# Gated three-branch decoder layer on one core: cross attention's scale moved to ScalarE, another PSUM bank for the index keys, split halves at the start, new product order, shifted tables

## The chip, the cores and the metric

The kernel runs on one core of a Trainium2 chip. TensorE multiplies (PE in the profile; PEld is its weight load), VectorE (DVE), ScalarE (ACT) and GpSimd (POOL) do elementwise work, and SyncE (SP) issues most transfers. The metric is the device time of one execution in microseconds, lower is better.

## What is computed

One decoder layer on 256 tokens of width 1024: h = rmsnorm(x), z = h @ w_in, and z is cut into the inputs of three mixers and their gates.

```
A: ya = moba_attention(rope(mq), rope(mk), mv)        8 heads of 64, causal
B: yb = dsa_attention(rope(dq), rope(dk), dv, index)  8 heads of 64; the index scores pick 64 keys per token
     score = sum over 8 index heads of relu(iq . ik / 8) * iw, causal; top 64
C: yc = cross_attention(xq, xk, xv)                   4 heads of 128 over 256 memory tokens
     xk, xv from rmsnorm(mem) @ w_mem_kv;  p = softmax(q . k / sqrt(128))
u   = sum over A, B, C of sigmoid(gate logits + b) * (w_up @ (y * silu(g)))
out = rmsnorm(x + u @ w_out)
```

With 256 tokens mixer A's past blocks are empty, so A is plain causal attention.

## The kernel before, in words

**Products.** Each fp32 operand is kept as a high part (a cast to fp32r) and a low part (the rest), and a product is three matmuls: high by high and the two mixed ones (`product`, L252 to L256). The work is a list of some 100 steps. A step is 512 KB of weights, computed in two halves, `mm(w, 0)` and `mm(w, 1)`, with side work allowed in the middle (the main loop, L988 to L1001). A step of `gemm` (blocks mv, i0, i1, dv, xv: 5 blocks of 4 steps) has the activations as PE's stationary operand, the weights as the moving one and two accumulators, one for each 128 tokens; a half step is 6 matmuls, three into the one accumulator, then three into the other. The other blocks (`gemm_k`, `gemm_t`, `gemm_kv`, `gemm_u`) hold the weights stationary. The program opens with steps 0 to 7, in which mv (even) and mq (odd) take turns.

**Weights.** For step s the SP queue loads `w{s}r` six steps ahead (four buffers; w3r goes on ACT's queue). `split_weights` (L240) makes the two parts three steps ahead: `w{s}h` is a cast on ACT (L248), `w{s}l` a subtraction on DVE (L249); five buffers of each. Steps 0 and 1 (`HALVED = 2`) are split in halves of 128x512, all others in one 128x1024 piece.

**Side work.** Attention, rotations, evacuations and normalisations stand at places in the list, as a step number with or without .5: `IDX` (index transpositions, index heads, top-k rounds), `TURNS` (load of a swapped copy and rotation of queries and keys), `M_PAIRS`, `D_PAIRS`, `X_HEADS` (heads of A, B, C), `GATES`, `MEM` (loads of the memory tokens), `LOAD_ROWS` (the token rows, for the norm), `ORDER` (the order of the weight blocks). The order of PE's and POOL's instructions is that of the program text. On ACT, DVE and SP a scheduler sets it from dependencies and places, so moving a place moves other instructions too.

**The parts touched.**

- `idx_transpose(t)` (L444), at steps 27.5 and 28.5. PE transposes the index queries in two groups of four (`iqt`, L454), ACT copies each to `iqT` (L455); then PE transposes the keys (`ikt`, L458) and DVE copies them to `ikT` (L459). All three PSUM tiles have the tag `sc`, which has two banks that are also used by attention scores (`msc`, `dsc`, `xsc`) and index heads (`lg`).
- `tp` is one bank, for the transpositions of probabilities: `mtp`, `dtp` (L626), `xpt` (L681).
- `self_values` (L641, `mya`): PE multiplies values by the transposed probabilities; their high part `mph` comes from ACT (L627), the low part `mpl` from DVE (L628). `self_scale` (L617) scales the probabilities `mpr` on POOL before they are transposed.
- `cross_scores` (L649): score, row maximum on DVE (L658, L659), two exponentials on ACT with row sums (L663). `cross_scale` (L669): reciprocal of the sums on DVE (L671), then a multiplication of each 128x256 half of `xpr` by it on POOL (L673). `cross_transpose` (L675): PE transposes to `xpt`. Four heads, so eight multiplications.

Of the kernel before, what the change touches and what calls it, by code (L numbers as in the profile page):

```python
# [9 lines left out]
F32R = mybir.dt.float32r  # L10
AF = mybir.ActivationFunctionType
# [3 lines left out]
P = 128  # L15
S = 256
# [46 lines left out]
HALVED = 2  # L63
ORDER = (
# [4 lines left out]
)  # L69
LOAD_ROWS = 1  # L70
X_STATS = 6

IDX = (27.5, 30, 35)

TURNS = (('mq', 8.5, 15.5), ('mk', 13.5, 20.5), ('dq', 28, 33), ('dk', 33, 36))

M_PAIRS = ((23, 25.5), (24, 27.5), (26.5, 29.5), (29.5, 31.5))
D_PAIRS = ((43.5, 47.5), (46.5, 49.5), (51.5, 53.5), (54.5, 55.5))
X_HEADS = (41.5, 44.5, 49, 50.5)
GATES = 59.5  # L80

MEM = (1.5, 6, 11, 15, 21.5)


def block_places(blocks, nk):
# [8 lines left out]
class Steps:  # L94
# [11 lines left out]
    def at(self, step, fn, *args):  # L106
        self.side[step].append((fn, args))
# [3 lines left out]
def hybrid_layer_kernel(  # L111
# [14 lines left out]
    nc = tc.nc  # L126
# [5 lines left out]
    psum = ctx.enter_context(tc.tile_pool(name="psum", bufs=1, space=bass.MemoryType.PSUM))  # L132
# [6 lines left out]
    def k4(nm, dt=F32):  # L139
        return keep.tile([P, 4, S], dt, name=nm, tag="t4", bufs=6)  # L140
# [99 lines left out]
    def split_weights(s):  # L240
        raw = loaded.pop(s)
        shape = list(raw.shape)
        hi = ws.tile(shape, F32R, name=f"w{s}h", tag="whi")
        lo = ws.tile(shape, F32R, name=f"w{s}l", tag="wlo")
        part = 1 if s < HALVED else shape[1]
        for j in range(0, shape[1], part):
            ks = slice(j, j + part)
            last_hi[0] = nc.scalar.copy(hi[:, ks, :], raw[:, ks, :]).ins  # L248
            nc.vector.tensor_sub(lo[:, ks, :], raw[:, ks, :], hi[:, ks, :].bitcast(F32))  # L249
        halves[s] = (hi, lo)  # L250

    def product(ps, a, b, first, last):  # L252
        (ah, al), (bh, bl) = a, b
        nc.tensor.matmul(ps, ah, bh, start=first, stop=False)
        nc.tensor.matmul(ps, ah, bl, start=False, stop=False)
        nc.tensor.matmul(ps, al, bh, start=False, stop=last)  # L256

    accs = {}
# [5 lines left out]
    def acc_tiles(nm):  # L264
        accs[nm] = [acc_bank(f"{nm}_{t}") for t in range(2)]

    def gemm(nm, act, src, place, nk=NK):

        off, n = place
        plan.first[nm] = len(plan.steps)  # L270
        for k0 in range(0, nk, 2):

            def mm(w, half, k0=k0):
                if k0 + half == 0:
                    acc_tiles(nm)
                a = act()
                for kk in (half,):
                    k = k0 + kk
                    for t in range(2):
                        tok = slice(t * P, (t + 1) * P)  # L280
                        product(
                            accs[nm][t][:, :n], (a[0](k, tok), a[1](k, tok)),
                            (w[0][:, kk, :], w[1][:, kk, :]), k == 0, k == nk - 1,
                        )

            plan.add((src, off, nk, n, k0, 2), mm)
        plan.end[nm] = len(plan.steps)
# [156 lines left out]
    def idx_transpose(t):  # L444
        if t == 0:
            idx["q"] = [k4(f"iqT{j}", F32R) for j in range(2)]
            idx["k"] = keep.tile([P, 2, S], F32R, name="ikT", tag="ikT")
            for nm in ("sel", "acc", "wk"):
                idx[nm] = keep.tile([P, 3 * P], F32, name=nm, tag=nm)
        tok = slice(t * P, (t + 1) * P)  # L450
        for j in range(2):
            tp = psum.tile([P, 4, P], F32R, name=f"iqt{t}{j}", tag="sc", bufs=2)
            for g in range(4):
                nc.tensor.transpose(tp[:, g, :], idx["qs", t][:, 4 * j + g, :], ident_r)  # L454
            nc.scalar.copy(idx["q"][j][:, :, tok], tp)  # L455
        tp = psum.tile([P, 2, S], F32R, name=f"ikt{t}", tag="sc", bufs=2)
        for j in range(2):
            nc.tensor.transpose(tp[:, j, 0:P], idx["ks", t][:, j, :], ident_r)  # L458
        nc.vector.tensor_copy(idx["k"][:, :, tok], tp[:, :, 0:P])  # L459
# [209 lines left out]
    def cross_scale(hd):  # L669
        pr, st = prs["x", hd]  # L670
        nc.vector.reciprocal(st[:, 4:6], st[:, 2:4])  # L671
        for t in range(2):
            nc.gpsimd.tensor_scalar_mul(pr[:, t, :], pr[:, t, :], st[:, 4 + t : 5 + t])  # L673

    def cross_transpose(hd):  # L675
        pr, _ = prs["x", hd]
# [178 lines left out]
    for t in range(2):  # L855
        at(IDX[0] + t, idx_transpose, t)
    for g in range(NH):
        at(IDX[1] + g / 2, idx_head, g)
    for r in range(TOPK // 8):
        at(IDX[2] + r, idx_round, r)  # L860
    at(IDX[2] + TOPK // 8, idx_select)
    for nm, swap, turn in TURNS:
        for hf in range(2):
# [7 lines left out]
    def attend(nm, starts, bias):  # L871
        for b, (s0, s1) in enumerate(starts):
            at(s0, self_scores, nm, b, bias)
            for e in range(2):
                at(s0 + 0.5 + 0.5 * e, self_scale, nm, 2 * b + e)
                at(s1 + e, self_transpose, nm, 2 * b + e)
                at(s1 + 1 + e, self_values, nm, 2 * b + e)

    attend("m", M_PAIRS, lambda: bias_c)
    attend("d", D_PAIRS, lambda: idx["sel"])  # L880

# [32 lines left out]

    at(LOAD_ROWS, load_rows)
    at(X_STATS, start_stats)
# [10 lines left out]

    for pair, s0 in enumerate(MEM[0:4]):
        at(s0, mem_load, pair)
# [4 lines left out]

    at(MEM[4], mem_stats)
    at(MEM[4] + 2, rstd_rows, m_rstd, mB, "mB")
    for hf in range(2):
# [3 lines left out]
    for hd, h0 in enumerate(X_HEADS):  # L941
        at(h0, cross_scores, hd)
        at(h0 + 0.5, cross_scale, hd)
        at(h0 + 2, cross_transpose, hd)
        at(h0 + 3.5, cross_values, hd)
# [16 lines left out]
    n = len(plan.steps)  # L962
# [18 lines left out]
    for s in range(-SPLIT_AHEAD, n):  # L981
        p, rest = divmod(s + SPLIT_AHEAD, 2)
        if p < 4 and not rest:
            first[p]()
        if s == 4:
            nc.sync.dma_start(cst, consts[:, 0:512])
            nc.sync.dma_start(tabT.rearrange("p t c -> p (t c)"), consts[:, 512:1024])
        for fn, args in plan.side.pop(s, []):  # L988
            fn(*args)
        if LOAD_AHEAD <= s + LOAD_AHEAD < n:  # L990
            load_weights(s + LOAD_AHEAD)
        if s + SPLIT_AHEAD < n:
            split_weights(s + SPLIT_AHEAD)
            if s + SPLIT_AHEAD == 0:
                load_late()
        if s >= 0:
            w = halves.pop(s)
            plan.steps[s][1](w, 0)
            for fn, args in plan.side.pop(s + 0.5, []):
                fn(*args)  # L1000
            plan.steps[s][1](w, 1)  # L1001
# [64 lines left out]
```

## Time and profile before

| | |
|---|---|
| runs, median (lowest to highest) | 330.37 us (329.61 to 330.69) |
| the profiled execution | 328.81 us, of which 327.0 us is the span of instructions |
| PE busy | 314.1 us, 96% of the span |
| DVE, ACT, POOL busy | 253.2 (77%), 199.3 (61%), 67.8 us (21%) |
| granted TensorE clock, mean | 0.994 |
| DMA | 59.45 MB, mean 182 GB/s |

The span is the time from the first to the last instruction in the trace; the 1.81 us between it and the execution's own time lie outside. A timeline row has start, duration, engine, line, operation, output and inputs, and in brackets the engine's idle time before it and what ended it. Matmuls overlap: the distance between two starts tells more than the duration.

### The profile page before, as it was taken

To read this page: it belongs to the slowest core of one execution; us is meant where nothing else is said; L and a number is where in the kernel's file an instruction comes from. 1 tells how busy PE (TensorE), PEld (TensorE's weight loads), DVE (VectorE), ACT (ScalarE), POOL (GpSimd) and SP (SyncE) were. 2 spreads that over 40 slices of the span, in tenths; PEclk is the share of its full clock that TensorE was granted. 3 is DMA by queue.
4 is the path that set the end of the run, shared out by engine and by line. 5 is a ranking of instruction groups with operands and counts; after the bars stand their busy time and mean duration, and the time that the engine had idled before them with its cause. 6 is when DMAs were issued, how large, how long until landed. Compare 5 with 4: busy or idle time off the path is not lost. (4 is left out here: it accounts for less than half of the span.)

```text
span 327.0 us, 6396 instructions
## 1 busy us (share of the span) xinstructions
PE 314.1 (96%) x2442; PEld 298.8 (91%) x2442; DVE 253.2 (77%) x456; ACT 199.3 (61%) x347; POOL 67.8 (21%) x66
## 2 busy tenths in 40 slices
PE   8899999999899999979999999999999999999992
PEld 7799999999799989869999998999999999999882
DVE  3579999998789999978766659999577677467523
ACT  5699565697777645275656586756444556644433
POOL 0001000039413000064423464231001011015011
PEclk9999999999999999999999999999999999999997
DMA  7998795846737266664434433468656666646003
GB/s 210 377 346 297 230 292 182 284 141 221 195 102 193 71 180 201 188 199 130 133 124 126 134 123 86 147 238 312 202 186 192 192 175 178 204 159 191 2 0 128
DMA packets 18368, 59.45 MB, mean 182 GB/s; under 512 B 2209, under 2 KB 2465, under 8 KB 18337
## 3 DMA queue, kind: packets, MB, share of 16 engines
q1 hardware_dynamic: 17760, 57.73, 56.1%
q10 hardware_dynamic: 576, 1.31, 1.1%
q8 instruction: 19, 0.31, 0.4%
q14 instruction: 13, 0.10, 0.1%
HBM read 55.89 MB, written 1.05 MB: 174 GB/s over the span
## 5 line engine op out<-in xcount | busy, mean ns | idle before, releaser
L617 POOL TENSOR_SCALAR mpr<-mpr,mst 128x128 f32<-128x128 f32 (+1 forms) x16 | 17.9, 1134 | 52.5 <-DVE mst L615 52.5
L744 POOL TENSOR_TENSOR u<-u,gt 128x512 f32<-128x512 f32 x7 | 10.7, 1529 | 76.0 <-DVE gt L741 76.0
L673 POOL TENSOR_SCALAR xpr<-xpr,xst 128x256 f32<-128x256 f32 x8 | 9.2, 1164 | 53.2 <-DVE xst L671 53.2
L617 POOL TENSOR_SCALAR dpr<-dpr,dst 128x128 f32<-128x128 f32 (+1 forms) x16 | 15.0, 956 | 16.2 <-DVE dst L615 16.2
L731 ACT ACTIVATE gt<-gt,x_first 128x256 f32<-128x256 f32 x24 | 10.9, 501 | 3.9 <-DVE gt L728 3.9
L607 ACT ACTIVATE dpr<-dms,dst 128x128 f32<-128x128 f32 (+1 forms) x16 | 7.1, 448 | 6.2 <-DVE dst L603 6.2
L663 ACT ACTIVATE xpr<-xsc,xst,xs_rstd 128x256 f32<-128x256 f32 x8 | 4.4, 561 | 6.9 <-DVE xst L659 6.9
L607 ACT ACTIVATE mpr<-mms,mst 128x128 f32<-128x128 f32 (+1 forms) x16 | 7.1, 445 | 1.8 <-DVE mst L603 1.8
L785 ACT ACTIVATE junk<-xn 128x512 f32<-128x512 f32 (+1 forms) x5 | 2.7, 543 | 8.6 <-DVE xn L783 8.6
L904 POOL COPY bias_c<-cst 128x128 f32<-128x128 f32 x1 | 1.0, 1037 | 25.5 <-DMA cst<-consts 25.5
L789 POOL TENSOR_TENSOR xn<-xn,gf 128x512 f32<-128x512 f32 x2 | 2.6, 1288 | 16.3 <-ACT junk L785 16.3
L749 ACT CAST us<-u 128x512 fp32r<-128x512 f32 x4 | 2.5, 622 | 5.1 <-POOL u L744 3.4
L485 ACT ACTIVATE rl<-lg 128x384 f32<-128x384 f32 x8 | 3.9, 484 | 2.7 <-issue 2.1
L647 DVE TENSOR_TENSOR dyT<-dyT,dya 64x256 f32<-64x256 f32 x8 | 3.3, 417 | 2.6 <-ACT dyT L646 2.5
L965 PE MATMUL warm<-ones 128*128 128x128 f32 x18 | 4.2, 430 | 1.0 <-DVE eps_t L960 1.0
L488 DVE SCALAR_TENSOR_TENSOR acc<-rl,iw,acc 128x128 f32<-128x128 f32 (+1 forms) x14 | 5.2, 414 | 0.0
L646 ACT COPY dyT<-dya 64x256 f32<-64x256 f32 x8 | 2.9, 366 | 3.6 <-PE dya L641 3.4
L603 DVE CUSTOM_DVE_ANT_0 mms<-msc,bias_c 128x128 f32<-128x128 f32 (+1 forms) x16 | 5.0, 348 | 0.0
L481 PE MATMUL lg<-ikT,iqT 128*128 128x128 f32 (+1 forms) x32 | 5.0, 278 | 0.0
L603 DVE CUSTOM_DVE_ANT_0 dms<-dsc,sel 128x128 f32<-128x128 f32 (+1 forms) x16 | 4.8, 354 | 0.2
L185 ACT ACTIVATE ehi<-eT,x_first 128x256 fp32r<-128x256 f32 x8 | 3.6, 505 | 2.1 <-DMA eT<-memT 2.1
L965 PEld LDWEIGHTS warm<-ones 128*128 128x128 f32 x18 | 3.9, 331 | 1.0 <-DVE eps_t L960 1.0
(1296 smaller groups left out, 1547.7 us busy)
## 6 DMA issues: line engine op xcount, KB each, us to landing
x_rows<-x SPq DMA_DIRECT2D x2, 512.0 KB, 6.9
eT<-memT SPq DMA_DIRECT2D x4, 256.0 KB, 4.6
xn<-x SPq DMA_DIRECT2D x2, 512.0 KB, 4.8
w0r<-w_in SPq DMA_DIRECT2D x2, 256.0 KB, 3.6
w1r<-w_in SPq DMA_DIRECT2D x2, 256.0 KB, 5.0
xT<-xT SPq DMA_DIRECT2D x2, 256.0 KB, 6.5
w2r<-w_in SPq DMA_DIRECT2D x1, 512.0 KB, 7.0
w3r<-w_in ACTq DMA_DIRECT2D x1, 512.0 KB, 7.0
```

The lines of the kernel that those rows point to most:

```text
L185: nc.scalar.activation(hi[:, k, :], src, AF.Copy, scale=g)
L481: nc.tensor.matmul(lg[:, c : c + n], q[:, q0:q1], idx["k"][:, j, 0:n], start=j == 0, stop=j == 1)
L485: nc.scalar.activation(rl, lg[:, : 3 * P], AF.Relu, scale=HD**-0.5)
L488: nc.vector.scalar_tensor_tensor(acc[:, c], rl[:, c], iw[:, t, g : g + 1], (bias_c if g == 0 else acc)[:, c], op0=OP.mult, op1=OP.add,)
L603: nc.vector.tensor_tensor_reduce(out=ms[:, c], in0=sc[:, c], in1=bias()[:, c], op0=OP.add, op1=OP.min, scale=-(HD**-0.5), scalar=3e38, acc ...
L607: big["last_exp"] = nc.scalar.activation(pr[:, c], ms[:, c], AF.Exp, bias=st[:, t : t + 1], scale=-1.0, accum_out=st[:, 2 + t : 3 + t],)
L617: nc.gpsimd.tensor_scalar_mul(pr[:, c], pr[:, c], st[:, 4 + t : 5 + t])
L663: big["last_exp"] = nc.scalar.activation(pr3[:, t, :], sc[:, t, :], AF.Exp, bias=st[:, t : t + 1], scale=xs_rstd[:, t : t + 1], accum_out= ...
L673: nc.gpsimd.tensor_scalar_mul(pr[:, t, :], pr[:, t, :], st[:, 4 + t : 5 + t])
L731: nc.scalar.activation(gt[:, f, :], gt[:, f, :], AF.Sigmoid, bias=x_first[:, j : j + 1])
L744: adder.tensor_tensor(u, u, gt, op=OP.add)
L965: nc.tensor.matmul(warm[:, 0:P], ones, ones, start=True, stop=True)
```

## The change

1. Cross attention's probabilities are scaled by ACT instead of POOL.
2. The PSUM tile `ikt` of the index keys takes the tag `tp` instead of `sc`.
3. The weights of steps 2 and 3 are split in halves, as those of 0 and 1 are.
4. In `gemm` a half step computes high by high for both accumulators, then high by low weights for both, then low by high weights for both.
5. Tables: the index work starts half a step (transpositions), one step (heads) and one and a half steps (rounds) earlier; rotations of dq come 3 steps earlier, of dk 1.5 later; the second and third pair of mixer B's heads start later by 1 and 0.5 and are transposed earlier by 0.5 and 0; the token rows are loaded 3 steps earlier, the memory's first two pairs later by 0.5 and 1; u20 comes after u03 and l22 before l23.

```diff
-LOAD_ROWS = 1
+LOAD_ROWS = -2
-IDX = (27.5, 30, 35)
+IDX = (27, 29, 33.5)
-D_PAIRS = ((43.5, 47.5), (46.5, 49.5), (51.5, 53.5), (54.5, 55.5))
+D_PAIRS = ((43.5, 47.5), (47.5, 49), (52, 53.5), (54.5, 55.5))
...
@@ split_weights
-        part = 1 if s < HALVED else shape[1]
+        part = 1 if s < HALVED + 2 else shape[1]
@@ gemm
-                for kk in (half,):
-                    k = k0 + kk
+                k = k0 + half
+                for i, (p, q) in enumerate(((0, 0), (0, 1), (1, 0))):
                     for t in range(2):
-                        tok = slice(t * P, (t + 1) * P)
-                        product(
-                            accs[nm][t][:, :n], (a[0](k, tok), a[1](k, tok)),
-                            (w[0][:, kk, :], w[1][:, kk, :]), k == 0, k == nk - 1,
+                        nc.tensor.matmul(
+                            accs[nm][t][:, :n], a[p](k, slice(t * P, (t + 1) * P)),
+                            w[q][:, half, :], start=k + i == 0, stop=k + i == nk + 1,
                         )
@@ idx_transpose
-        tp = psum.tile([P, 2, S], F32R, name=f"ikt{t}", tag="sc", bufs=2)
+        tp = psum.tile([P, 2, S], F32R, name=f"ikt{t}", tag="tp", bufs=1)
@@ cross_scale
-            nc.gpsimd.tensor_scalar_mul(pr[:, t, :], pr[:, t, :], st[:, 4 + t : 5 + t])
+            nc.scalar.activation(
+                pr[:, t, :], pr[:, t, :], AF.Copy, scale=st[:, 4 + t : 5 + t]
+            )
```

What the tables move is seen in the order of the instructions, at three places.

PE, first index transposition (`iqt`, `ikt`), before: it stands behind the first half of step 27 of block dk0.

```order
L254 MATMUL dk0ps<-xhi,w27h 128x256
L255 MATMUL dk0ps<-xlo,w27h 128x256
L256 MATMUL dk0ps<-xhi,w27l 128x256
L454 MATMUL iqt_1167<-ident_r,iqs_931 128x128 x4
L454 MATMUL iqt_1173<-ident_r,iqs_931 128x128 x4
L458 MATMUL ikt_1179<-ident_r,iks_932 128x128 x2
L641 MATMUL mya_1085<-mph_1092,mv 128x256
L641 MATMUL mya_1085<-mpl_1093,mv 128x256
L641 MATMUL mya_1085<-mph_1092,mv 128x128
L641 MATMUL mya_1085<-mpl_1093,mv 128x128
L626 MATMUL mtp_1191<-cst,mpr_977 128x128 x3
L254 MATMUL dk0ps<-xhi,w27h 128x256
```

Now it stands ahead of step 27:

```order
L254 MATMUL dk0ps<-xhi,w26h 128x256
L255 MATMUL dk0ps<-xlo,w26h 128x256
L256 MATMUL dk0ps<-xhi,w26l 128x256
L453 MATMUL iqt_1150<-ident_r,iqs_935 128x128 x4
L453 MATMUL iqt_1156<-ident_r,iqs_935 128x128 x4
L457 MATMUL ikt_1162<-ident_r,iks_936 128x128 x2
L254 MATMUL dk0ps<-xhi,w27h 128x256
L255 MATMUL dk0ps<-xlo,w27h 128x256
L256 MATMUL dk0ps<-xhi,w27l 128x256
```

The transposition of the index moved by one half step, away from the product `mya` and the transposition `mtp` of mixer A, which it used to precede directly.

DVE, around the first low part `mpl` of mixer A's probabilities, which PE's `mya` reads (`w..l` are low parts of weights, `mst` row sums), before:

```order
L249 TENSOR_TENSOR w27l<-w27r,w27h 128x1024
L615 RECIPROCAL mst_976<-mst_976 128x2
L249 TENSOR_TENSOR w28l<-w28r,w28h 128x1024
L615 RECIPROCAL mst_983<-mst_983 128x2
L628 TENSOR_TENSOR mpl_1045<-mtp_1046,mph_1044 128x384
L249 TENSOR_TENSOR w29l<-w29r,w29h 128x1024
L249 TENSOR_TENSOR w30l<-w30r,w30h 128x1024
L647 TENSOR_TENSOR myT<-myT,mya_1085 64x256
L628 TENSOR_TENSOR mpl_1093<-mtp_1094,mph_1092 128x384
```

and now:

```order
L249 TENSOR_TENSOR w28l<-w28r,w28h 128x1024
L614 RECIPROCAL mst_980<-mst_980 128x2
L614 RECIPROCAL mst_987<-mst_987 128x2
L249 TENSOR_TENSOR w29l<-w29r,w29h 128x1024
L627 TENSOR_TENSOR mpl_1049<-mtp_1050,mph_1048 128x384
L249 TENSOR_TENSOR w30l<-w30r,w30h 128x1024
L646 TENSOR_TENSOR myT<-myT,mya_1089 64x256
L627 TENSOR_TENSOR mpl_1097<-mtp_1098,mph_1096 128x384
```

The low part of step 29's weights went ahead of `mpl`; that of step 27 now stands 27 rows ahead of that of step 28.

ACT, around the first head of cross attention (`xpr` its probabilities, `w..h` casts of weights), before:

```order
L248 CAST w45h<-w45r 128x1024
L663 ACTIVATE xpr_1863,xst_1860<-xsc_1853,xst_1860,xs_rstd 128x256 x2
L248 CAST w46h<-w46r 128x1024
L248 CAST w47h<-w47r 128x1024
L607 ACTIVATE dpr_1929,dst_1928<-dms_1927,dst_1928 128x128
L685 CAST xph_1946<-xpt_1941 128x512
```

and now:

```order
L248 CAST w45h<-w45r 128x1024
L248 CAST w46h<-w46r 128x1024
L662 ACTIVATE xpr_1875,xst_1872<-xsc_1865,xst_1872,xs_rstd 128x256 x2
L248 CAST w47h<-w47r 128x1024
L672 ACTIVATE xpr_1875<-xpr_1875,xst_1872 128x256 x2
L606 ACTIVATE dpr_1933,dst_1932<-dms_1931,dst_1932 128x128
L686 CAST xph_1950<-xpt_1945 128x512
```

The cast of step 46 went ahead of the two exponentials (L663, now L662), and the two multiplications that POOL did (L673, now L672 on ACT) stand behind the cast of step 47. On DVE the reciprocal that they read now stands behind the low part of step 46, where it stood between those of 45 and 46.

## Rows read from the trace of the kernel before

**Rows 1.** The page, section 1: busy us, share of the span, instructions.
```profile
PE 314.1 (96%) x2442; PEld 298.8 (91%) x2442; DVE 253.2 (77%) x456; ACT 199.3 (61%) x347; POOL 67.8 (21%) x66
```

**Rows 2.** Waits of PE, whole span: total us, times, longest.
```profile
PE xpt L681 <- POOL xpr L673: 2.1, 1, 2.1
PE ikt L458 <- ACT iqT L455: 1.5, 2, 1.2
...
PE mv_0ps L255 <- DVE w2l L249: 0.8, 1, 0.8
...
PE mv_0ps L254 <- ACT w2h L248: 0.3, 1, 0.3
...
PE dtp L626 <- DVE xpl L686: 0.2, 1, 0.2
```

**Rows 3.** Timeline of ACT: start, us, line, operation, idle before and releaser.
```profile
8.77 0.62 ACT L248 CAST w1h<-w1r 128x512 fp32r<-128x512 f32 x1 [0.99 <-DMA w1r<-w_in]
...
11.04 1.05 ACT L248 CAST w2h<-w2r 128x1024 fp32r<-128x1024 f32 x1 [0.42 <-DMA w2r<-w_in]
13.73 1.05 ACT L248 CAST w3h<-w3r 128x1024 fp32r<-128x1024 f32 x1 [1.64 <-DMA w3r<-w_in]
...
19.23 1.05 ACT L248 CAST w6h<-w6r 128x1024 fp32r<-128x1024 f32 x1
```

**Rows 4.** Timeline of DVE, 6 to 20 us.
```profile
9.42 0.69 DVE L249 TENSOR_TENSOR w1l<-w1r,w1h 128x512 fp32r<-128x512 f32 x1 [0.92 <-ACT w1h L248]
...
12.12 1.23 DVE L249 TENSOR_TENSOR w2l<-w2r,w2h 128x1024 fp32r<-128x1024 f32 x1 [0.98 <-ACT w2h L248]
```

**Rows 5.** Timeline of PE, 11.5 to 16.2 us.
```profile
11.60 0.28 PE L256 MATMUL mq_1ps<-xhi,w1l 128*128 128x256 f32 x1
12.14 0.50 PE L254 MATMUL mv_0ps<-w2h,xhi 128*128 128x512 f32 x1 [0.26 <-ACT w2h L248]
13.40 0.50 PE L255 MATMUL mv_0ps<-w2l,xhi 128*128 128x512 f32 x1 [0.76 <-DVE w2l L249]
13.73 0.40 PE L256 MATMUL mv_0ps<-w2h,xlo 128*128 128x512 f32 x1
13.97 0.40 PE L254 MATMUL mv_1ps<-w2h,xhi 128*128 128x512 f32 x1
...
16.07 0.28 PE L254 MATMUL mq_0ps<-xhi,w3h 128*128 128x256 f32 x1
```

**Rows 6.** Windows, step 3: busy by engine, then PEclk, DMA share, GB/s.
```profile
16.07:18.87 2.80, 2.80 (x25) 2.80 (x24) 2.68 (x5) 2.80 (x6) 0.00 (x0) 1.00 1.00 404
```

**Rows 7.** Timeline of DVE, 67 to 84 us.
```profile
75.86 0.53 DVE L628 TENSOR_TENSOR mpl<-mtp,mph 128x384 fp32r<-128x384 f32 x1
76.32 1.21 DVE L249 TENSOR_TENSOR w29l<-w29r,w29h 128x1024 fp32r<-128x1024 f32 x1
```

**Rows 8.** Timeline of PE, 75 to 90 us.
```profile
76.49 0.35 PE L641 MATMUL mya<-mpl,mv 128*128 128x256 f32 x1
...
83.04 0.37 PE L458 MATMUL ikt<-ident_r,iks 128*128 128x128 f32 x2 [1.15 <-ACT iqT L455]
```

**Rows 9.** Timeline of DVE, 137 to 146 us.
```profile
137.95 0.16 DVE L659 TENSOR_TENSOR xst<-xst,xs_rstd 128x2 f32<-128x2 f32 x1
138.01 1.23 DVE L249 TENSOR_TENSOR w45l<-w45r,w45h 128x1024 fp32r<-128x1024 f32 x1
...
139.46 0.17 DVE L671 RECIPROCAL xst<-xst 128x2 f32<-128x2 f32 x1
```

**Rows 10.** Tile xpr: durations in ns, least/median/most.
```profile
L673 POOL TENSOR_SCALAR xpr<-xpr,xst x8: 922/925/2589, 139.7 to 175.4; 128x256 f32<-128x256 f32 x8
```

**Rows 11.** ACT groups by line and form: count, busy us, mean ns.
```profile
L731 ACT ACTIVATE gt<-gt,x_first 128x256 f32<-128x256 f32 x24 | 10.9, 501 | 3.9 <-DVE gt L728 3.9
```

**Rows 12.** Timeline of PE, 139.5 to 144.2 us.
```profile
143.52 0.55 PE L681 MATMUL xpt<-cst,xpr 128*128 128x128 f32 x3 [2.10 <-POOL xpr L673]
```

**Rows 13.** Tile mpr on POOL: durations in ns, least/median/most.
```profile
L617 POOL TENSOR_SCALAR mpr<-mpr,mst x16: 601/961/2412, 68.8 to 99.9; 128x128 f32<-128x128 f32 x8, 128x256 f32<-128x256 f32 x8
```

More of the change, by code (lines that the diff above doesn't have):

```diff
@@ L66 @@
     "xv", "mg0", "mg1", "dg0", "dg1", "xg0", "xg1", "l10", "l01", "l00", "u00", "l02", "u10",
[2 rows of a table removed]
[2 rows of a table added]
 )
-LOAD_ROWS = 1
+LOAD_ROWS = -2
 X_STATS = 6
-IDX = (27.5, 30, 35)
-TURNS = (('mq', 8.5, 15.5), ('mk', 13.5, 20.5), ('dq', 28, 33), ('dk', 33, 36))
+IDX = (27, 29, 33.5)
+TURNS = (('mq', 8.5, 15.5), ('mk', 13.5, 20.5), ('dq', 27, 30), ('dk', 34, 37.5))
 M_PAIRS = ((23, 25.5), (24, 27.5), (26.5, 29.5), (29.5, 31.5))
-D_PAIRS = ((43.5, 47.5), (46.5, 49.5), (51.5, 53.5), (54.5, 55.5))
+D_PAIRS = ((43.5, 47.5), (47.5, 49), (52, 53.5), (54.5, 55.5))
 X_HEADS = (41.5, 44.5, 49, 50.5)
 GATES = 59.5
-MEM = (1.5, 6, 11, 15, 21.5)
+MEM = (2, 7, 11, 15, 21.5)
 def block_places(blocks, nk):
```

4 rows, old and new, of the table ORDER are left out of this document.

## The prediction

> **What bounds the kernel now.** I began with the busy times [rows 1]: PE works 314.1 of 327.0 us, 96%, and no other engine is above 77%. So the time is what PE has to do, plus the stretches in which it stands. Work added to or taken from DVE, ACT or POOL counts only where PE waits for it. The second view is therefore the list of PE's waits [rows 2]: one for POOL's scaled probabilities of cross attention (2.1 us), two for ACT's copy of the transposed index queries (1.5), two on the weights of step 2 (0.8 for the low part, 0.3 for the high one), one of 0.2 ahead of a transposition of mixer B. These 4.9 us are the most that taking waits away can bring; everything else on PE is work, and the change leaves its amount alone: the same matmuls in another order. The third step was to open the timelines around each wait and put the new order into them. All times below are in the coordinates of the trace before.
>
> **The change part by part.**
>
> *Split halves and new product order (start).* Weights of step 2 land at 11.01, since the cast that waits for them starts at 11.04 [rows 3]. Cast and subtraction take the whole 512 KB: PE can start at 12.14 [rows 5], the low part begins at 12.12 and takes 1.23 [rows 4], and PE stands again until 13.40. Step 2 ends at 16.07 instead of 11.60 + 0.12 + 2.80 = 14.52 (a step of PE takes 2.80 [rows 6], a 256-column product 0.12): 1.55 us are lost there. In halves, a cast takes 0.62 and a subtraction 0.69 [rows 3, 4]: the first half's high part is there at 11.66, its low part at 12.37. The new order lets both high-by-high products, 2 x 0.23, run in between, from 11.72 to 12.19, so PE stands about 0.2 and then has 10 products left: 12.40 + 10 x 0.233 = 14.73. That is 1.34 earlier. Then step 3 becomes the next that is late: its weights land at 13.71 [rows 3], cast 14.35, low part 15.06, while the first product with a low part is due at 14.73 + 2 x 0.12 = 14.97; about 0.12 is given back. Gain **1.2**. Bounds: 1.55 if nothing is late, 0 if another load comes later instead (below). The halves' extra time on ACT and DVE (2 x 0.62 against 1.05, 2 x 0.69 against 1.23, twice) is 0.7 us in all, spread over a stretch in which both wait for transfers (0.42 and 1.64 us ahead of the two casts [rows 3]); without that cover the weights of step 4 would be 0.7 late.
>
> *Token rows earlier in the load queue.* On SP's queue the second half of the token rows now stands ahead of w6r. At 404 GB/s [rows 6] its 512 KB delay w6r by 1.3 us. The cast of w6 began at 19.23 [rows 3]; with 1.3 more, cast and subtraction end at 19.23 + 1.3 + 1.05 + 1.23 = 22.8. Step 6 is due at 16.07 + 3 x 2.80 - 1.2 = 23.3. Hidden, with 0.5 us to spare, so at nothing.
>
> *Product order elsewhere.* `gemm` has 240 matmuls in 20 steps; the accumulator changed every third matmul (80 times) and now changes with every one (240), 160 more. Low end: within mv the change from mv_0 to mv_1 took 13.97 - 13.73 = 0.24 [rows 5], and the nine products from 13.97 to 16.07, with two more changes among them, 0.233 each: nothing to be seen. High end: the slowest step from one product to the next there, after a wait, is 13.73 - 13.40 = 0.33, 0.09 more, 14 us for 160 of them. I take 0, because the row with a change of accumulator in it is the nearest. Gain 0.
>
> *Index keys in another bank, index work half a step earlier.* The keys' transposition stood 1.15 us [rows 8] and once more the rest of the 1.5 [rows 2], until ACT had copied a tile of the two-bank tag. In `tp` it needs no such copy. Both waits go: 1.5. But DVE now has the low part of step 29's weights (1.21) ahead of `mpl`, which ran from 75.86 to about 76.3 [rows 7], while PE's `mya` reads it at 76.49 [rows 8]. It moves to about 77.0 to 77.45: a new wait of **1.0**. Behind it on PE stand the rest of `mya`, `mtp` and the next scores of mixer A, and DVE, which reads those, comes later with them. Sharing the one bank of `tp` adds nothing: half a step of products (1.4, half of [rows 6]) now stands between `ikt` and the next `mtp`, and DVE's copy of 128x256 is shorter than the 0.53 for 128x384 [rows 7]. Net 0.5 (bounds 0, if POOL's `mpr` is late too, and 1.5).
>
> *Cross attention's scale on ACT.* Before: row maximum scaled at 137.95 on DVE, exponentials, reciprocal at 139.46 [rows 9], then POOL twice, one of the two slowed to 2.59 against a median of 0.92 [rows 10]; PE goes on at 143.52 after 2.10 [rows 12]. In the new order DVE does the low parts of steps 45 and 46 behind the row maximum, 138.01 + 2 x 1.2, then the reciprocal, 140.6. ACT has done the exponentials and the cast of step 47 by then (139.4 + 1.05) and scales at 0.5 each [rows 11], done at about 141.7. PE goes on at 141.8, **1.7** earlier. PE still waits there, from about 141.4, for a chain that runs over DVE and ACT. That wait swallows what PE gained in the index stage alone, so the 0.5 of the last part does not add. The startup gain does: there the splits, which DVE and ACT do at PE's pace, move along. Bounds: 0.7 if DVE's chain is late by one more split (1.2, less what the index stage saved), 2.1 + 0.5 if it is not on the path. The other seven multiplications had no wait of PE behind them [rows 2], and the 8 x 0.5 = 4 us on ACT lie on an engine that is 61% busy [rows 1].
>
> *Mixer B's pairs.* The 0.2 us wait of `dtp` for DVE [rows 2] goes, since its scores and so its place move by half a step: **0.2** (bounds 0 and 0.2).
>
> *The rest of the tables* (order of u20 and l22, rotations, memory loads, later rounds) touches stretches in which PE has no wait in the list, and each moved load is still asked for steps ahead: 0.
>
> **Sum:** 1.2 + 1.7 + 0.2 = 3.1 us, of 4.9 us of waits. The profiled execution took 328.81 us (span 327.0 and 1.81 around it): 325.7. The median of the runs, 330.37, is 1.56 above that execution, and I keep the difference: **327.3 us**.
>
> **The rivals.**
>
> *New waits in the index stage.* POOL's `mpr` took 0.6 at least and 2.41 at most [rows 13], so something slows it by up to 1.8. In the new order the subtractions of steps 28 and 29 stand back to back on DVE just when POOL scales the second head, and `mtp` waits for that. If it is held over one more subtraction for each of two heads, PE loses 2 x 1.2 there. The 0.5 that the index stage gains, and some 0.7 of PE's remaining wait at `xpt`, absorb 1.2 of it: gain 3.1 - 1.2 = 1.9, 328.5 us. For it: the 2.59 of [rows 10] fell beside two such subtractions. Against it: PE's list has no wait for `mpr` now.
> The Trainium skill, "SBUF — State Buffer", section "Who interferes with whom", says that a VectorE instruction with two SBUF inputs contends with a GpSimd instruction that reads SBUF, and that the one that comes second is blocked for the whole of the other. By that rule the held `mpr` above is the normal case, and the move of `xpr` to ScalarE, which by the same section waits for nobody, is right. The slow rows agree with it in size; that no wait of PE came of it before is why I leave this a rival.
>
> *The startup gain is not handed on.* Either w6r is later than I think, or the chain ahead of `xpt`, on a DVE that is 77% busy, does not move along with PE. Then 1.2 is lost: gain 1.9, 328.5 us. For it: DMA's share is 1.00 at the start [rows 6]; against it: 0.5 us to spare.
>
> *The alternating accumulators cost time (slower).* One mechanism: each of the 160 additional changes of accumulator and stationary operand in mv, i0, i1, dv and xv makes PE step later. It decides from (3.1 + 1.0) / 160 = 26 ns per change, where the kernel would be measurably slower; at half of the high end, 45 ns, it costs 7.2: 330.37 - 3.1 + 7.2 = 334.5 us. Against it stand the 0.233 per product across three changes [rows 5] and the granted clock of 1.00 in the busy stretch [rows 6].
> The Trainium skill, "TensorE: Matmul & The Clock Gate", section "A second HAM failure mode: psum-queue depth-cycling", tells of a kernel that cycled through PSUM banks, made small pauses and had its clock go up and down. Here the clock stays at its upper level (2.4 GHz) in a stretch that changes bank every third matmul; no run yet shows it with every one.
>
> *More than forecast.* `mpl` is not late and PE gets to `xpt` when it is ready: up to 1.2 + 1.5 + 2.1 + 0.2 = 5.0 us, 325.4 at the far end.
>
> **How the numbers follow.** A measurement of this kernel tells about 0.3% from no change, 0.99 us: faster is below 329.4, slower above 331.4. Chances: forecast 0.54, more than forecast 0.08, index stage 0.19, startup 0.13, accumulators 0.06. The forecast's own range is 326.4 to 328.3. The first two are faster. Index stage and startup, at 328.5 with an uncertainty of about 1 us and able to come together (0.7 left of the gain), are half faster and half the same. So faster 0.62 + 0.16 = 0.78, same 0.16, slower 0.06. The range leaves out the accumulators, most of the two rivals coming together and the far end of "more": 325.6 to 329.4.
>
> **What would show it.** In the list of PE's waits: `xpt` for POOL gone and one of up to 1 us on ACT's scale or none in its place; both `ikt` waits gone, one of about 1.0 at `mya` for `mpl`; the waits on w2 down to about 0.2; step 4 starting some 1.2 earlier. The pitch of mv's products should still be 0.23. Wrong would be: a wait for POOL's `mpr` at `mtp`, a wait for w6l, a clock below 1.00, a pitch above 0.25, or a wait at `xpt` as long as before.

## The result, and the profile after

The changed kernel takes **325.88 us** (median of 4 runs, 324.03 to 326.02) against 330.13 for the kernel before beside it; ratio 0.986, 95% interval 0.982 to 0.990. Six more runs later gave a median of 324.89, and all 80 runs of the kernel before in this study average 329.7, all ten of the changed one 325.2: a gain of 4.5 us. I had forecast 3.1, to 327.3; the result lies below the forecast's own range of 326.4 to 328.3. The sign and most of the places were right; the size was not, and the profiled executions alone do not show why: there the spans differ by 327.0 - 324.2 = 2.8 us.

The page of the changed kernel, engines, answering to [rows 1]:

```profile
PE 314.7 (97%) x2442; PEld 299.5 (92%) x2442; DVE 252.8 (78%) x458; ACT 202.8 (63%) x357; POOL 55.0 (17%) x58
```

POOL gave 12.8 us away, ACT took 3.5. The waits of PE, answering to [rows 2]:

```profile
PE warm L966 <- DVE eps_t L961: 1.0, 1, 1.0
PE mya L640 <- DVE mpl L627: 0.9, 1, 0.9
PE dya L640 <- DVE dyT L646: 0.7, 1, 0.7
PE mv_0ps L280 <- ACT w2h L248: 0.3, 1, 0.3
PE xpt L682 <- ACT xpr L672: 0.2, 1, 0.2
```

`xpt` fell from 2.1 to 0.2, both `ikt` waits and the wait on w2's low part are gone, and the new wait of 0.9 at `mya` is there.

**Start.** Timeline of ACT, answering to [rows 3], then of PE, to [rows 5] (L280 is `gemm`'s matmul):

```profile
11.36 1.14 ACT L248 CAST w2h<-w2r 128x512 fp32r<-128x512 f32 x2 [0.68 <-DMA w2r<-w_in]
14.17 1.14 ACT L248 CAST w3h<-w3r 128x512 fp32r<-128x512 f32 x2 [1.67 <-DMA w3r<-w_in]
```

```profile
12.03 0.50 PE L280 MATMUL mv_0ps<-w2h,xhi 128*128 128x512 f32 x1 [0.33 <-ACT w2h L248]
12.37 0.40 PE L280 MATMUL mv_1ps<-w2h,xhi 128*128 128x512 f32 x1
12.76 0.50 PE L280 MATMUL mv_0ps<-w2l,xhi 128*128 128x512 f32 x1
13.09 0.40 PE L280 MATMUL mv_1ps<-w2l,xhi 128*128 128x512 f32 x1
...
15.20 0.28 PE L254 MATMUL mq_0ps<-xhi,w3h 128*128 128x256 f32 x1
...
18.25 0.40 PE L280 MATMUL mv_0ps<-w4h,xhi 128*128 128x512 f32 x1
```

In this execution the weights of steps 2 and 3 landed 0.3 and 0.4 us later than in the first profile of before, so step 4, which began at 18.87 there, comes only 0.62 earlier. From the cast of w3 to step 4 it is 4.08 us, before 18.87 - 13.73 = 5.14.

**Index stage.** Timeline of DVE, answering to [rows 7], and of PE, to [rows 8]:

```profile
75.26 1.20 DVE L249 TENSOR_TENSOR w29l<-w29r,w29h 128x1024 fp32r<-128x1024 f32 x1
76.39 0.54 DVE L627 TENSOR_TENSOR mpl<-mtp,mph 128x384 fp32r<-128x384 f32 x1
```

```profile
76.98 0.38 PE L640 MATMUL mya<-mpl,mv 128*128 128x256 f32 x1 [0.91 <-DVE mpl L627]
```

From the start of step 26 to that of step 34 PE took 37.85 us before and takes 37.77 now: hardly a gain.

**First cross head.** Timelines of DVE, ACT and PE, answering to [rows 9], [rows 11] and [rows 12]:

```profile
138.87 1.22 DVE L249 TENSOR_TENSOR w46l<-w46r,w46h 128x1024 fp32r<-128x1024 f32 x1
140.00 0.15 DVE L670 RECIPROCAL xst<-xst 128x2 f32<-128x2 f32 x1
```

```profile
139.00 1.05 ACT L248 CAST w47h<-w47r 128x1024 fp32r<-128x1024 f32 x1
140.19 0.91 ACT L672 ACTIVATE xpr<-xpr,xst 128x256 f32<-128x256 f32 x2
```

```profile
140.75 0.95 PE L682 MATMUL xpt<-cst,xpr 128*128 128x128 f32 x4 [0.24 <-ACT xpr L672]
```

The scale takes 0.91 for both halves on ACT. Step 43, with `xpt` inside, lasted 6.59 us before (138.72 to 145.31) and 4.86 now: 1.73 saved, 1.7 forecast. The tile's durations, answering to [rows 10], no longer spread as they did on POOL (922 to 2589 ns):

```profile
L672 ACT ACTIVATE xpr<-xpr,xst x8: 493/504/512, 140.2 to 174.2; 128x256 f32<-128x256 f32 x8
```

The Trainium skill, "SBUF — State Buffer", section "Who interferes with whom", has ScalarE wait for no other engine's use of the memory; these eight, beside a busy DVE, agree.

By stages the two traces give: start 0.62, steps 4 to 42 with the index stage 0.03, step 43 with the first cross head 1.73, steps 44 to 57 0.37; sum 2.75. The other 1.7 of the 4.5 had to come from something that the first profiled execution of before did not contain.

### The profile page after: what moved, and what is told of

Same layout as the page of the kernel before. It is cut to its first block, busy times and chain, and to the rows that moved or that the text cites. A ratio compares the mean times of both kernels' runs of the same rounds, so it can differ in the third digit from the quotient of the medians.

```text
span 324.2 us, 6395 instructions
## 1 busy us (share of the span) xinstructions
PE 314.7 (97%) x2442; PEld 299.5 (92%) x2442; DVE 252.8 (78%) x458; ACT 202.8 (63%) x357; POOL 55.0 (17%) x58
## 3 DMA queue, kind: packets, MB, share of 16 engines
HBM read 55.89 MB, written 1.05 MB: 176 GB/s over the span
## 4 chain that ended last, share of the span: by engine, by line
PE 71%; DVE 15%; issue 4%; ACT 4%; DMA 2%; POOL 1%; SPq 1%; DVEq 0%; ACTq 0%; POOLq 0%
DMA w2r<-w_in 2%; PE i_0ps L280 2%; PE i_1ps L280 2%; DVE wk L498 2%; PE mv_0ps L280 1%; PE mv_1ps L280 1%; DVE m L496 1%; PE o_0ps L255 1%; PE o_0ps L254 1%; PE o_0ps L256 1%; POOL dpr L616 1%; PE dya L640 1%; PE lg L480 1%; PE o_1ps L256 1%; PE o_1ps L255 1%
## 5 line engine op out<-in xcount | busy, mean ns | idle before, releaser
L616 POOL TENSOR_SCALAR mpr<-mpr,mst 128x128 f32<-128x128 f32 (+1 forms) x16 | 15.9, 1009 | 54.7 <-DVE mst L614 54.7
L745 POOL TENSOR_TENSOR u<-u,gt 128x512 f32<-128x512 f32 x7 | 9.9, 1412 | 77.1 <-DVE gt L742 77.1
L662 ACT ACTIVATE xpr<-xsc,xst,xs_rstd 128x256 f32<-128x256 f32 x8 | 4.4, 560 | 3.3 <-DVE xst L658 3.3
L627 DVE TENSOR_TENSOR dpl<-dtp,dph 128x384 fp32r<-128x384 f32 x8 | 4.4, 554 | 0.4
L626 ACT CAST dph<-dtp 128x384 fp32r<-128x384 f32 x8 | 3.8, 479 | 1.4 <-PE dtp L625 1.3
L784 DVE TENSOR_TENSOR xn<-o_0ps,xn 128x512 f32<-128x512 f32 x2 | 1.4, 692 | 4.2 <-PE o_0ps L256 4.2
```

The costliest lines, as they stand in the source:

```text
L616: nc.gpsimd.tensor_scalar_mul(pr[:, c], pr[:, c], st[:, 4 + t : 5 + t])
L745: adder.tensor_tensor(u, u, gt, op=OP.add)
```

## The experiments

Two theories stood against each other. One: the waits are worth what the trace shows, and the rest is scatter of the first transfers. The other: one of the waits costs more in most executions than it did in the profiled one.

**The kernel before again** (no edit).

> The kernel before, unchanged, as a second profiled execution. Theory 1 (the difference of 1.5 us between the first profiled execution, 328.81, and the median of the runs, 330.1, is the scatter of the first transfers' landing): the profile's time lies between 328.5 and 331, and what it is longer than 328.81 stands ahead of step 8, with w2r or w3r landing that much later; waits behind that as before (xpt 2.1, ikt 1.5). Theory 2 (there is a wait that the first profile did not happen to show, and the change takes it away): an additional wait of about 1.5 us stands somewhere behind step 8.

Measured: ratio 1.0005 (0.9965 to 1.0044), the profile at 330.16 us. The start is 0.11 earlier than in the first profile, and the waits are the same, but from the start of step 45 on it is 1.4 later. Windows of the new profile, columns as in [rows 6]:

```profile
141.00:143.00 2.00, 0.28 (x3) 0.09 (x1) 2.00 (x5) 0.31 (x2) 2.00 (x1) 1.00 0.85 244
143.00:145.00 2.00, 1.63 (x8) 1.42 (x9) 1.14 (x7) 1.39 (x6) 0.31 (x1) 0.94 0.93 340
145.00:147.00 2.00, 2.00 (x10) 1.85 (x9) 0.98 (x4) 2.00 (x8) 1.50 (x3) 0.50 0.37 147
147.00:149.00 2.00, 2.00 (x14) 2.00 (x14) 0.93 (x2) 1.00 (x2) 1.48 (x3) 0.71 0.00 0
149.00:151.00 2.00, 2.00 (x19) 2.00 (x18) 1.89 (x3) 0.68 (x1) 0.00 (x0) 1.00 0.00 0
```

and of the first profile of before:

```profile
145.00:147.00 2.00, 2.00 (x18) 1.91 (x17) 0.98 (x4) 2.00 (x8) 1.34 (x2) 1.00 0.49 201
```

PE waits 2.09 us for POOL in both (the windows at 141 show how little it did), goes on, and in the new profile, about 1.4 us later, its granted clock falls from 1.00 to 0.50, the lower of its two levels (1.2 instead of 2.4 GHz), for some 3.4 us: 10 matmuls in the window at 145 instead of 18. Steps 43 and 44 together take 12.32 us instead of 10.79, **1.5 more**. So the wait at `xpt` has a second price, which the first profile happened not to show. Each run lists its mean granted clock too: of the 76 executions of the kernel before in this study for which it is listed, 36 have 0.992 or less and average 330.3 us, 40 have more and average 329.1. The line between them is not sharp: six executions at 0.993, a value that no kernel without the wait shows, average 330.4, and with them it is 42 of 76 and a difference of 1.5 us. So about half of them pay. Theory one falls; theory two fits, with the clock and no second wait as what was missing.

**The scale on ScalarE alone.**

```diff
@@ cross_scale, in the kernel before
-            nc.gpsimd.tensor_scalar_mul(pr[:, t, :], pr[:, t, :], st[:, 4 + t : 5 + t])
+            nc.scalar.activation(pr[:, t, :], pr[:, t, :], AF.Copy, scale=st[:, 4 + t : 5 + t])
```

> Before with cross attention's scaling on ScalarE alone. By the trace of before the reciprocal stands at 139.46, ACT is free after the cast of step 46 at 140.3 and scales until 141.3, PE is there at 141.4: the wait of 2.1 at xpt goes whole, gain 2.1 us (328.0), more than the 1.73 that the whole change won there, since the tables put the reciprocal behind one more split. Rival (POOL's slow multiplication was only the visible end of DVE's queue): PE still waits 0.5 or more for ACT there, gain at most 1.6. Rival (hidden wait): gain 3 or more.

Measured: 327.62 us, ratio 0.9932 (0.9895 to 0.9968). The wait at `xpt` is gone whole (step 43 takes 4.28 instead of 6.59 us, 2.3 less), and in none of 8 executions is the mean clock at 0.992 or less. Of the 2.3, step 44 gives 1.0 back: the products of `xya` come to DVE's low part of the values (`xvl`) before it is there, which the wait at `xpt` had hidden. The first of these pauses:

```profile
147.25 0.38 PE L256 MATMUL xya<-xph,xvl 128*128 128x256 f32 x1 [0.29 <-DVE xvl L574]
```

Of the 2.1 us between the medians, 1.3 is then waiting (steps 43 and 44 take 9.52 us instead of 10.79) and some 0.6 clock (1.3 us in half the executions). The interval, 1.1 to 3.5 us, holds the rivals' figures as well; it is the trace that speaks against both, as no wait of 0.5 is left at `xpt` and no other long wait of PE went with it.

**Halves and product order alone.**

```diff
@@ in the kernel before
-        part = 1 if s < HALVED else shape[1]
+        part = 1 if s < HALVED + 2 else shape[1]
...
@@ gemm: the new product order, as in the change
```

> Before with the halves of steps 2 and 3 and the new product order alone. Stage theory: gain 0.6 (as between the two traces) to 1.2 (my sum) at the start; the scheduler then puts the low part of step 29 ahead of mpl, a new wait of 0.9 at mya, which the wait of 2.1 at xpt swallows; gain at the end 0.6 to 1.2 (about 329.2). Pitch of mv's products still 0.23. Rival (alternating accumulators cost time): pitch above 0.25, no gain. Rival (hidden wait is at the start): gain 2 or more.

Measured: 328.99 us, ratio 0.9973 (0.9936 to 1.0009), so about 0.8 us, not clear of nothing. In the trace step 4 starts 1.84 earlier (1.0 by the halves; the rest is w3, which landed 0.8 earlier in this execution), `mya` then waits 0.9 for `mpl`, and steps 26 to 34 take 38.84 us instead of 37.85:

```profile
PE xpt L680 <- POOL xpr L672: 2.1, 1, 2.1
...
PE mya L640 <- DVE mpl L627: 0.9, 1, 0.9
```

One part of the expectation failed: the wait of 2.1 at `xpt` did not swallow the loss at `mya`. It is as long as before, with the clock down behind it, and step 43 starts only 0.83 earlier, 1.84 less the 1.0 lost. The chain ahead of `xpt` moved along with PE. mv's products keep a pitch of 0.233.

**The tables alone**, everything else as before.

> The new tables alone, with POOL's scaling, the old tag, the old splits and product order. Stage theory: the reciprocal of the first cross head stands behind one more split, POOL starts 1.1 later and the wait at xpt grows from 2.1 to about 3; the ikt wait of 1.1 stays; the dtp wait of 0.2 and some of the small waits in mixer B go: between 0.3 faster and 1 slower. Rival (the tables carry the unexplained 1.5 us): 1.5 faster or more.

Measured: 330.15 us, ratio 1.0015 (0.9977 to 1.0053), as expected: no gain by themselves. The waits at the first `xpt` did not grow to 3, they are 2.2 in two pieces, and 5 of 10 executions have the low clock. Not expected is the index stage: steps 26 to 34 take 38.77 us, 0.9 more than before, with longer waits at `ikt`:

```profile
PE ikt L458 <- ACT iqT L455: 1.8, 2, 0.9
```

**Filling the wait.**

```diff
@@ cross_transpose, in the kernel before
         tp = psum.tile([P, 512], F32, name=f"xpt{hd}", tag="tp", bufs=1)
+        if hd == 0:
+            for _ in range(16):
+                nc.tensor.matmul(tp[:, 0:S], acts["x"][0][:, 0, 0:P], acts["x"][0][:, 0, :],
+                                 start=True, stop=True)
```

> Before, with 16 products of 128x256 that nobody reads put in front of the first xpt (into its own tile, which the transpositions then overwrite), so that PE works about 1.9 of the 2.1 us that it waits there. No useful work is saved, and everything else stands as in before. Clock theory: xpt starts at the same 143.5, the granted clock stays 1.00 behind it, and the runs are 0.7 to 1.4 us faster than before (ratio 0.996 to 0.998), without the executions of 331 us. Rival (the clock falls for another reason, or its fall costs the end nothing): ratio 1.000, clock at 0.5 behind xpt in the profile.

Measured: 328.95 us; ratio 0.999 (0.9965 to 1.0014), a smaller gain than expected and by itself not clear of nothing. The trace is clear. Windows behind the filled stretch:

```profile
143.00:145.00 2.00, 1.86 (x14) 1.54 (x13) 1.55 (x10) 1.48 (x7) 1.11 (x2) 1.00 0.81 256
145.00:147.00 2.00, 2.00 (x16) 1.82 (x15) 1.27 (x3) 2.00 (x6) 2.00 (x4) 1.00 0.69 260
```

Steps 43 and 44 take 10.80 us, as in the first profile of before, with 16 more matmuls in them. None of 12 executions has a mean clock of 0.992 or less, against 10 of 23 of the kernel before beside them, and their mean, 329.0, is that of the kernel before's 13 executions with the clock up, also 329.0. So work that nobody needs keeps the clock up. On average that should be worth 0.7 us (1.6 us in 10 of 23 executions); the medians differ by 0.6. One execution still took 330.94, with its clock up, so not every slow execution has this cause.

**The changed kernel again** (no edit).

> The changed kernel again, with more runs. Theory (in the kernel before, PE's wait of 2.1 us at the first xpt often makes the granted clock fall to half for about 3 us, which costs 1.4 us more, and the first profiled execution of before was one in which it did not fall): here PE waits 0.2 there, the clock stays at 1.00 in all windows but the last, and the ratio to before is 0.986 to 0.990 (3.3 to 4.6 us). Rival (the scatter of the runs alone made the first ratio): 0.990 to 0.993, as the 2.8 us between the first two profiles.

Measured: 324.89 us, ratio 0.9865 (0.9831 to 0.9899). In this profile step 4 starts at 17.74, 1.13 earlier than in the first profile of before; everything behind is as in the first profile of the change within 0.03 us at step 58, and the clock is 1.00 until the last 2 us.

**The scale back on GpSimd.**

```diff
@@ cross_scale, in the changed kernel
-            nc.scalar.activation(pr[:, t, :], pr[:, t, :], AF.Copy, scale=st[:, 4 + t : 5 + t])
+            nc.gpsimd.tensor_scalar_mul(pr[:, t, :], pr[:, t, :], st[:, 4 + t : 5 + t])
```

> The changed kernel with cross attention's scaling back on POOL. Theory: the reciprocal stays behind the low part of step 46, POOL starts then, and the subtraction of step 47 slows one of its two multiplications: PE's wait at xpt is 2.3 or more instead of 0.2, and the clock falls behind it in most executions: 2.3 to 3.7 us slower than the changed kernel, near the time of before (328.5 to 330). Rival (the tables and the start carry most of the gain): at most 1 us slower than the changed kernel.

Measured: 328.16 us, ratio 0.9956 (0.9924 to 0.9989), 3.3 slower than the changed kernel beside it. Its first wait and two windows:

```profile
PE xpt L680 <- POOL xpr L672: 2.2, 2, 1.6
```

```profile
144.00:146.00 2.00, 2.00 (x7) 1.56 (x6) 0.93 (x3) 2.00 (x8) 0.68 (x2) 0.54 0.48 197
146.00:148.00 2.00, 2.00 (x13) 2.00 (x12) 1.41 (x2) 1.81 (x3) 2.00 (x3) 0.61 0.00 0
```

The mean clock is at 0.992 or less in 5 of 10 executions, in half and not in most. Over all kernels of this study: of 57 executions of kernels without the wait of about 2 us at `xpt`, none; of 106 of kernels with it, 51.

**The index keys back in the two-bank tag.**

```diff
@@ idx_transpose, in the changed kernel
-        tp = psum.tile([P, 2, S], F32R, name=f"ikt{t}", tag="tp", bufs=1)
+        tp = psum.tile([P, 2, S], F32R, name=f"ikt{t}", tag="sc", bufs=2)
```

> The changed kernel with the index keys' transposition back in the two-bank tag. Two waits on ACT's copy of the queries return at ikt. Theory (in the index stage DVE is the bound, 98% busy, so PE's waits there only change places): ikt waits about 1 us in all, and of it at most 0.5 us is still there at step 34; steps 25 to 34 take 37.8 to 38.3 us (37.77 in the changed kernel, 37.85 before). Rival (my sum: the two waits are worth 1.5 us): steps 25 to 34 take 39 us or more.

(The two figures given there, 37.85 and 37.77, run from the start of step 26 to the start of step 34; so does the one measured.) Measured: 39.15 us for the stretch, 326.29 us in all, ratio 0.9902 (0.987 to 0.9933).

```profile
PE ikt L457 <- ACT iqT L454: 1.5, 2, 0.9
PE mya L640 <- DVE mpl L627: 1.1, 1, 1.1
...
PE xpt L682 <- ACT xpr L672: 0.2, 1, 0.2
```

The rival was right: inside the change the bank is worth 1.4 us, and DVE is not the only bound there. The loss goes on to the end: the wait at `xpt` and step 43 (4.87 us) are as in the changed kernel, and the runs are 1.1 to 1.4 us slower than those of the changed kernel (mean 326.3 against 325.2, median against 324.89). What takes the bank's gain away again are the tables and the product order: without the bank they make the stage 1.3 us longer than before (39.15 against 37.85). The bank alone, on the kernel before, was not run.

**The new product order in mv alone.**

```diff
@@ gemm, in the changed kernel
...
+                seq = [(i, t) for i in range(3) for t in range(2)]
+                if nm != "mv":
+                    seq = [(i, t) for t in range(2) for i in range(3)]
...
```

> The changed kernel, with the new product order in mv alone (i0, i1, dv and xv keep the old one). The order of DVE then has mpl ahead of the low part of step 29 again. Theory: the wait of 0.9 at mya goes; of it 0.3 to 1.0 us reach the end, the rest comes back as a longer wait at xpt, which was 0.2. If xpt's chain over DVE and ACT does not move along, PE waits about 1.2 there and the time is as for the changed kernel. Rival (the new order in i0, i1, dv, xv itself costs or saves time on PE): the pitch of dv and xv products differs from 0.233.

Measured: 325.12 us, ratio 0.9874 (0.9844 to 0.9904), the changed kernel's time. The 1.1 us that `mya` lost beside its normal 0.47 are gone from the trace, but steps 26 to 34 take 37.70 us, only 0.07 less:

```profile
PE ikt L461 <- DVE mpl L631: 0.5, 1, 0.5
...
PE iqt L457 <- DVE mst L606: 0.2, 1, 0.2
```

PE comes to the index transpositions earlier and waits there, for a bank that the next `mpl` frees (the one of `tp`) and for scores that DVE has still to read: 0.7 in this list, in place of 0.9 at `mya`. With the run before this says: the two-bank tag cost 1.4, and behind it stands DVE's queue, which holds PE back in one place or the other.

**Whole splits with the new order; halves with the old order.**

```diff
@@ split_weights, in the changed kernel (the first)
-        part = 1 if s < HALVED + 2 else shape[1]
+        part = 1 if s < HALVED else shape[1]
@@ gemm, in the changed kernel (the second): the old product order, as before
```

> The changed kernel with steps 2 and 3 split whole again, the new product order kept. Both high-by-high products of step 2 run before the wait for the low part, so the product order alone is worth 0.23: between step 2's landing (start of its cast) and the start of step 4 lie 7.8 - 0.2 = 7.6 us, against 7.8 before and 6.9 in the changed kernel. Rival (the order alone does it): 7.1 or less.

> The changed kernel with the old product order everywhere, the halves kept. Step 2 then waits for the first half's low part behind one product instead of two, 0.2 more than the changed kernel, and step 3 hides part of that: from the start of step 2's cast to the start of step 4 6.9 to 7.1 us. The low part of step 29 goes behind mpl on DVE, so the wait of 0.9 at mya goes; steps 25 to 34 stay within 0.3 us of the changed kernel's 37.77. Rival (alternating accumulators cost or save): the whole kernel 0.5 us or more faster or slower than the changed kernel.

Measured: 326.41 us (0.9906, 0.9869 to 0.9943) and 325.72 (0.9887, 0.9847 to 0.9928). The start is best read as distances from the casts, which begin as the weights land:

| kernel | cast of w2 to step 3 | cast of w3 to step 4 |
|---|---|---|
| before | 5.03 | 5.14 |
| whole splits, new order | 4.80 | 5.04 |
| halves, old order | 4.07 | 4.08 |
| changed kernel | 3.84 | 4.08 |

The new order is worth 0.23 on step 2, with halves or without. On step 4 it is worth nothing in the kernels with halves, since the landing of w3, 2.5 to 3.2 us after that of w2, sets it. The halves are worth 1.0. My expectations counted from w2's cast and so mixed in w3's landing; by that count (8.26 and 7.07 us) the first missed. The steps with the old order are as long as with the new: from step 28 to step 58, which holds dv and xv, the second kernel takes 113.69 us and the changed one 113.70. The second kernel's four runs are 0.5 us above the mean of the changed one's ten, which is the rival's figure; the intervals of the two ratios overlap, and no stage of its trace shows such a loss.

**Loads of w2 and w3 in two transfers each**, with the new product order in mv alone.

```diff
-    load_weights(2)
+    load_weights(2, 0)
+    load_weights(2, 1)
...
-            load_weights(3, queue=nc.scalar)
+            load_weights(3, 0, nc.scalar)
+            load_weights(3, 1, nc.scalar)
```

> A version that is to beat both: the changed kernel with the new product order in mv alone, and the loads of w2 and w3 each issued as two transfers of 256 KB, so that the first half of each lands some 0.6 us earlier than the whole did. Theory (what is left of the start is the wait for these two landings): PE does not wait for w2h any more (0.3 to 0.4 in the changed kernel), step 4 starts 0.3 to 0.7 us earlier, 324.5 us or a ratio of 0.984. Rival (the transfers share the queues' bandwidth, so that the first half lands hardly earlier than the whole): step 4 starts as in the changed kernel, 17.7 to 18.3.

Measured: 325.23 us, ratio 0.9876 (0.9842 to 0.9911): no better than the changed kernel. The first halves land earlier (w2 at 10.51, w3 at 12.42), PE does not wait for them, and step 4 starts at 17.40, the earliest but one. Then steps 4 and 5 take 3.09 and 3.04 us instead of 2.80, since PE stands for their low parts. The cast of w4, and so its low part, stands behind that of w3's second half, which landed no earlier than the whole did; the cast of w5 stands behind the squares of the token rows on ACT.

```profile
14.37 0.62 ACT L248 CAST w3h<-w3r 128x512 fp32r<-128x512 f32 x1 [1.30 <-DMA w3r<-w_in]
```

So no version here beats the changed kernel measurably.

## Why the prediction was wrong in size

- **The clock: the step that failed.** "The median of the runs, 330.37, is 1.56 above that execution, and I keep the difference". The sum took this difference over to the changed kernel, and it did not stay: there the median of the runs is 0.14 below the profiled execution (325.88 against 326.02). In part it was the clock's fall behind the 2.1 us wait, 1.3 to 1.5 us in about half of the executions of before, and in none of the changed kernel, since the wait is gone. That is 0.6 to 0.8 of the mean. The sum priced the wait at its length and put the clock at nothing, from the one execution that was profiled. The cue was there: three of three runs above the profiled execution, and a wait of 2.1 us, the longest of PE. The rest of the difference is how single executions lie, the profiled one of before below the mean of those with the clock up (328.81 against 329.1), that of the changed kernel above its mean (326.02 against 325.2).
- **Start, 1.2 forecast: nearly right**, 1.0 to 1.1 at equal landing (the table above), although the first pair of traces shows 0.62. The product order's 0.23 on step 2, which the sum counted, does not reach step 4, since w3's landing sets that. The gain is handed on: step 43 begins 0.65 earlier.
- **First cross head, 1.7: right**, 1.73. DVE's reciprocal and ACT's scale came in the order and, with 0.65 added for the earlier step 43, within 0.1 us of the times of the sum.
- **Index stage, net 0.5 that `xpt` swallows: wrong twice, and without effect by luck.** The bank is worth 1.4 (1.5 forecast) and the new wait at `mya` costs 1.1 (1.0), but the tables, which the sum put at nothing here, cost 0.9 when they stand alone, and of the 0.5 less than 0.1 was left. Nor does `xpt` swallow anything: what the stage loses without the bank, or with halves and product order alone, comes out behind `xpt`, and the wait there keeps its length, because the chain ahead of it moves along with PE. Leaving out the 0.5 came right only because there was no gain to add. And the one bank of `tp` does add a wait: 0.2 at `ikt` for `mpl` in the later profile of the changed kernel and 0.5 with the new order in mv alone.
- **Mixer B, 0.2:** the wait of `dtp` is gone; steps 44 to 57 are 0.37 shorter, and where the other 0.17 comes from stays open.
- **Rivals.** Alternating accumulators cost nothing: mv's pitch stayed 0.233, the order back in four blocks changed nothing, and in the changed kernel the clock stayed at 1.00 through all blocks that alternate. The bank cycling that the Trainium skill describes ("TensorE: Matmul & The Clock Gate", "A second HAM failure mode: psum-queue depth-cycling") does not show here. POOL's `mpr` held nobody up, nor did w6r. "More than forecast" came true through a mechanism that it did not name.

In sum 1.05 + 0.03 + 1.73 + 0.37 + 0.6 = 3.8 us are accounted for, of 4.5 measured (4.0 with the clock at 0.8); with the interval of the later ratio (0.983 to 0.990, 3.3 to 5.6 us) the rest may be scatter, and it stays open.

## What to carry to other kernels

One profile shows one execution: where it lies below all the timed runs, look for what the others have and it has not, and profile the same kernel again before pricing a wait. A long wait of TensorE costs its own length and, with some chance, a stretch at the lower clock behind it; so the longest wait deserves the first edit, and its length in one trace may be less than its price. A wait that is removed from a stage with two bounds moves to the second: undo the edit alone to see its worth, not the whole.

## What the runs showed of the hardware

- Behind a wait of about 2 us (2.1 us in one piece, or 1.6 and 0.6) the granted clock fell to 0.50 for 3.4 us, in four of five profiles of kernels with such a wait, from about its end to 1.4 us later. By the mean clock it fell in about half of the executions, and never in kernels whose wait there was 0.3 us or less, or was filled with idle products.
- From about 202 us on, PE runs at one of two paces, at the same granted clock of 1.00: 682 or 688 matmuls in 80 us, 117.8 or 116.7 ns for a product of 256 columns, 0.9 us over the rest (from step 58 to the end 124.7 or 123.8 us). Seven of the 14 profiles have the slow one. First the kernel before again, then halves and product order alone:

```profile
210.00:290.00 80.00, 80.00 (x682) 80.00 (x681) 57.91 (x57) 45.13 (x59) 8.95 (x6) 1.00 0.64 202
```

```profile
210.00:290.00 80.00, 80.00 (x688) 80.00 (x687) 58.00 (x57) 44.42 (x59) 8.95 (x6) 1.00 0.65 205
```

What sets it was not tried. Both kernels that were profiled twice had the slow pace both times, so the profiles alone do not tell whether it goes by the execution or by the kernel; kernels whose one profile has the fast pace (mv's product order, two transfers) did not run faster than the changed kernel, whose two have the slow one.
- The landing of w3 varied from 12.9 to 14.4 us between the profiles of kernels that load it in one transfer, and PE's start of step 4 followed it within 0.2 us, at 5.04 to 5.25 us behind the cast of w3 with whole splits and 4.08 to 4.15 with halves.
